# The opening's squares, the constants' conversion and the early products of a fp32 decoder layer, put in another order

## The chip, the cores and the metric

One NeuronCore of a Trainium2 chip runs the whole layer as one program. The time is that of one execution on the device, in microseconds (us). Five engines work beside each other, each through its own queue in program order, and wait for one another by semaphores: PE (TensorE, matrix products; PEld is its loading of weights), DVE (VectorE), ACT (ScalarE), POOL (GpSimd) and SP (SyncE, which here only issues DMAs). POOL issues some DMAs too.

## What is computed

A decoder layer on x of 1024 positions by 1024 features, all in fp32, with a D_FF of 2816:

```
x = x + 0.5 * swiglu_ffn(rmsnorm(x, ffn1_norm), ffn1_w_gate, ffn1_w_up, ffn1_w_down)
x = x + hybrid_mixer(rmsnorm(x, mix_norm), ...)      # NSA attention + gated linear attention
x = x + 0.5 * swiglu_ffn(rmsnorm(x, ffn2_norm), ffn2_w_gate, ffn2_w_up, ffn2_w_down)
return rmsnorm(x, final_norm)

swiglu_ffn(x, w_gate, w_up, w_down) = (silu(x @ w_gate) * (x @ w_up)) @ w_down
rmsnorm(x, g) = x * rsqrt(mean(x * x) + EPS) * g
```

## The kernel before

**Products.** Each fp32 product is three matmuls on rounded halves (`mm3`, L193 to L195: high by high, high by low, low by high). A weight tile is brought from DRAM to `raw` by SP (L407 for the early ones), its high half is made by ACT (L433) and its low half by DVE (L436). Making weights is a `step` of the walk over the list of products, which looks up to four products ahead (`LOOK`).

**FFN.** The hidden features are worked through in 22 tiles of 128. For each the up and gate products over two halves of x (positions and features both cut in two) are formed by a scheme of Strassen's kind: seven products of 12 matmuls each, of sums and differences of the weights (S1 to S4, DVE) with sums and differences of the halves of x (T1 to T4). One of the seven, A12 by B21, needs only features 4 to 7 of x in half 0 of the positions, multiplied by the gain but not yet by the norm; so these **early products** are done for all 22 tiles ahead of the tiles. The result of each is copied by ACT from PSUM to a half of `kept` (even and odd tiles alternate, L612), stored by SP to the DRAM buffer `pd` (L546), and brought back (`recall`, L546 too) when its tile comes, where DVE adds it (L640) to the snapped A11 product `hf`. A copy to a half of `kept` waits until the store that reads that half has landed.

**Opening.** While the early products run, ACT and DVE make the norm of x: eight squares for each half of the positions (ACT L248), added up by DVE (L252, the last one L257), summed over the partitions by PE (L268), then v (DVE L273), its power of -0.5, r (POOL L275), and r spread over the partitions by PE (L280); for half 0 ACT copies that to SBUF (`rb`, L1934). Then DVE scales x in place (16 times, L304), the halves of x are made (ACT L312 the highs, DVE L313 the lows), and `combine` makes the differences (DVE L334) for T2, T3, T1 and T4 and their halves. All this is a side generator (`first`): it gets one tick behind each k-step of a product, that is behind every 3 matmuls, and a table `due` of ticks says when the steps of the norm are emitted; `PACE` sets how fast the combinations follow. What one engine does in which order is thus settled by the order in which the code emits it.

**FFN2.** Its opening is emitted in the mixer's last loop over the output (`ot`, L2149 adds to x, L248 squares, L2158 stores x to `xs`), with the early weights loaded by `ahead` and a `step` at two of the places.

**Constants.** `round_consts` has POOL convert two DRAM tables of 2.1 MB each (`qx`, `bias`) to the rounded type by DMA from DRAM to DRAM (L114). They are needed in the mixer.

## Time and profile before

| | |
|---|---|
| median of 3 runs | 1945.82 us (1945.74 to 1947.72) |
| the profiled execution | 1946.0 us, span 1944.2 us |
| PE busy | 1909.6 us, 98% of the span |
| DVE, ACT, POOL busy | 70%, 46%, 11% |
| matmuls | 9291 |
| granted TensorE clock, mean | 0.993 |

In the rows of the timeline and of the groups the first number is the start in us, the second the time in us (busy time for a group), then engine, line, operation, output <- inputs by the program's names, tile shapes, and xN for N instructions in a row. In brackets: how long the engine was idle just before, and whose end it waited for. Lines are those of the kernel before. In the table of DMA issues the last number is the median from issue to landing.

### The profile page before, as it was taken

Reading aid. Unit: us, or ns where it says so; the run is one execution under the profiler, and the core shown is the slowest. Engines: PE = TensorE matmul, PEld = TensorE weight load, DVE = VectorE, ACT = ScalarE, POOL = GpSimd, SP = SyncE. Lnnn points to the kernel's source line nnn. Section 1 sums busy time; section 2 is a strip of 40 time slices with the busy share of each in tenths; the row PEclk is TensorE's granted clock in tenths of the full one; section 3 lists DMA queues with packets and bytes.
Section 4 is the critical chain, followed back from the end, with each engine's and each line's share of the span. In section 5 each row is a group of like instructions: output and inputs, shape, how many; then the busy total and the mean of one; then the engine's idle time right before and its main releaser. Section 6 shows DMA issues by size and latency. Waiting matters only on the chain.

```text
span 1944.2 us, 26337 instructions
## 1 busy us (share of the span) xinstructions
PE 1909.6 (98%) x9291; PEld 1569.5 (81%) x9291; DVE 1370.5 (70%) x2292; ACT 898.1 (46%) x1717; POOL 219.8 (11%) x251
## 2 busy tenths in 40 slices
PE   8899999999999999999999999999999999999998
PEld 6788888888888888778877888878788888888887
DVE  6887778886776763454867887457777777767766
ACT  5533333344444552323479887235433333344443
POOL 0000000000000010121467654000000000000001
PEclk9999999999999999999999999999999999999999
DMA  8533345559874330118353422635333455588652
GB/s 292 186 131 127 128 152 193 192 195 335 298 254 163 124 102 27 53 46 243 128 168 94 148 71 93 227 122 192 125 130 130 152 195 195 195 308 284 237 177 87
DMA packets 173588, 325.53 MB, mean 167 GB/s; under 512 B 17712, under 2 KB 49072, under 8 KB 173136
## 3 DMA queue, kind: packets, MB, share of 16 engines
q1 hardware_dynamic: 165296, 308.87, 46.8%
q0 software_dynamic: 2304, 10.23, 1.6%
q10 hardware_dynamic: 5856, 4.75, 0.8%
q8 instruction: 73, 1.20, 0.2%
q14 instruction: 59, 0.48, 0.1%
HBM read 234.75 MB, written 93.39 MB: 169 GB/s over the span
## 4 chain that ended last, share of the span: by engine, by line
PE 88%; DVE 4%; ACT 3%; DMA 3%; issue 1%; POOL 1%; SPq 0%; ACTq 0%; POOLq 0%; DVEq 0%
PE bank L193 23%; PE bank L194 23%; PE bank L195 23%; PE pair L1431 3%; PE bank L1503 3%; PE bank L963 2%; PE bank L965 2%; PE bank L964 2%; PE bank L1521 1%; PE bank L1522 1%; DMA raw<-in_w_f_dram 1%; ACT p L1472 1%; DMA pd<-kept 1%; PE bank L1156 0%; PE pair L1439 0%
## 5 line engine op out<-in xcount | busy, mean ns | idle before, releaser
L193 PE MATMUL bank<-T,wt 128*128 128x512 f32 x704 | 275.0, 391 | 7.0 <-ACT hf L612 6.6
L194 PE MATMUL bank<-T,wt 128*128 128x512 f32 x704 | 274.6, 390 | 0.0
L195 PE MATMUL bank<-T,wt 128*128 128x512 f32 x704 | 274.5, 390 | 0.0
L193 PE MATMUL bank<-bd,wd 128*128 128x512 f32 (+1 forms) x632 | 243.1, 385 | 0.0
L195 PE MATMUL bank<-bd,wd 128*128 128x512 f32 (+1 forms) x632 | 242.6, 384 | 0.0
L194 PE MATMUL bank<-bd,wd 128*128 128x512 f32 (+1 forms) x632 | 242.5, 384 | 0.0
L193 PE MATMUL bank<-h,wt 128*128 128x512 f32 x528 | 208.0, 394 | 0.5 <-ACT wt L433 0.5
L195 PE MATMUL bank<-h,wt 128*128 128x512 f32 x528 | 206.7, 392 | 0.4 <-DVE wt L436 0.3
L194 PE MATMUL bank<-h,wt 128*128 128x512 f32 x528 | 206.7, 391 | 0.0
L275 POOL TENSOR_TENSOR r<-v,mhalf 128x4 f32<-128x4 f32 (+1 forms) x9 | 10.4, 1159 | 1355.2 <-DVE v L273 1355.2
L612 ACT ACTIVATE g<-bank 128x512 f32<-128x512 f32 x88 | 52.7, 598 | 236.3 <-PE bank L195 236.3
L193 PEld LDWEIGHTS bank<-T,wt 128*128 128x128 f32 x704 | 132.6, 188 | 35.7 <-ACT hf L612 7.5
L195 PEld LDWEIGHTS bank<-T,wt 128*128 128x128 f32 x704 | 132.6, 188 | 27.6
L194 PEld LDWEIGHTS bank<-T,wt 128*128 128x128 f32 x704 | 132.6, 188 | 27.6
L433 ACT ACTIVATE wt<-v 128x512 fp32r<-128x512 f32 x176 | 109.9, 624 | 76.7 <-PE bank L195 50.9
L193 PEld LDWEIGHTS bank<-bd,wd 128*128 128x128 f32 x632 | 118.8, 188 | 23.5
L195 PEld LDWEIGHTS bank<-bd,wd 128*128 128x128 f32 x632 | 118.7, 188 | 23.4
L194 PEld LDWEIGHTS bank<-bd,wd 128*128 128x128 f32 x632 | 118.8, 188 | 23.2
L193 PE MATMUL bank<-h,w 128*128 128x512 f32 x320 | 127.2, 398 | 0.0
L195 PE MATMUL bank<-h,w 128*128 128x512 f32 x320 | 124.9, 390 | 0.0
L436 DVE TENSOR_TENSOR wt<-v,wt 128x512 fp32r<-128x512 f32 x176 | 120.6, 685 | 6.0 <-ACT wt L433 5.6
L194 PE MATMUL bank<-h,w 128*128 128x512 f32 x320 | 124.7, 390 | 0.0
(279 smaller groups left out, 3883.8 us busy)
## 6 DMA issues: line engine op xcount, KB each, us to landing
in<-in_w_f_dram SPq DMA_DIRECT2D x132, 256.0 KB, 5.4
in<-b SPq DMA_DIRECT2D x132, 256.0 KB, 5.4
raw<-in_w_f_dram SPq DMA_DIRECT2D x44, 512.0 KB, 4.6
up<-in_w_f_dram SPq DMA_DIRECT2D x44, 512.0 KB, 5.3
raw<-in_w_in_dram SPq DMA_DIRECT2D x23, 512.0 KB, 4.0
raw<-in_w_f_dram SPq DMA_DIRECT2D x44, 256.0 KB, 3.9
pd<-kept SPq DMA_DIRECT2D x44, 256.0 KB, 2.2
kept<-pd SPq DMA_DIRECT2D x44, 256.0 KB, 5.7
```

What stands on the lines that cost most here:

```text
L193: mm(ps, w[0], x[0], start=first, stop=False, skip_group_check=True)
L194: mm(ps, w[0], x[1], start=False, stop=False, skip_group_check=True)
L195: mm(ps, w[1], x[0], start=False, stop=last, skip_group_check=True)
L433: nc.scalar.activation(t[:, 0], a, AF.Copy)
L436: nc.vector.tensor_tensor(t[:, 1], a, t[:, 0].bitcast(F32), OP.subtract)
L612: nc.scalar.activation(dst, src, AF.Copy)
L963: mm(p, a, w[:, 0, c], start=f, stop=False, skip_group_check=True)
L964: mm(p, a, w[:, 1, c], start=False, stop=False, skip_group_check=True)
L965: mm(p, b, w[:, 0, c], start=False, stop=l, skip_group_check=True)
L1431: nc.tensor.matmul(s[:, i + c, :w], Q[:, j, r], kk[br, g][:, k0:k0 + w], start=(j == 0 and i % per == 0), stop=False, skip_group_check=True)
L1472: nc.scalar.activation(p[:, i].rearrange("p (c w) -> p c w", c=nch), sv[:, i * nch:i * nch + nch], AF.Exp, bias=nm[:, i:i + 1], accum_out= ...
L1503: nc.tensor.transpose(t[:, r * 128:r * 128 + 128], heads[r][:, k * 128:k * 128 + 128], self.ident)
```

## The change

- **Opening.** `begin` takes two steps of weights more and then emits six of the eight squares of half 0 ahead of the first products; the other two come at the side generator's ticks 1 and 2. The squares of half 1 begin at tick 20 instead of 10. The steps of the norm come at ticks 19, 23, 31 and 35 (before: 18, 22, 25 and 29), the scalings and combinations from tick 27 on (before 24). `PACE` goes from 1.35 to 1.3. For the first two products the look-ahead is three.
- **Constants.** `round_consts` is called 16 times, behind the A22 products of tiles 4 to 19, each time for an eighth of `qx` or `bias`. Ahead of each DMA POOL copies a column of the weights of a tile five ahead into a fifth column of `mhalf`, so that the DMA, behind the copy in POOL's queue, is issued once these weights have landed. Before, the two DMAs were written behind tile 10's A22, but no operand made them wait.
- **Early products.** They go through tiles 2 to 21 and then 0 and 1 (`head`). The results of tiles 0 and 1 stay in `kept`: they are not stored to `pd` and not brought back.
- **FFN2.** `ahead(0)` and `ahead(1)` are called behind `ot` 5 and `ahead(2)` behind `ot` 7; before, `ahead(0)` behind 5 and the other two behind the loop.

```diff
 AHEAD2 = 12
-PACE = 1.35
+PACE = 1.3
...
         self.gains = self.const.tile([128, 4, KT], F32, name="gains")
-        self.mhalf = self.const.tile([128, 4], F32, name="mhalf")
+        self.mhalf = self.const.tile([128, 5], F32, name="mhalf")
         self.blank = self.const.tile([128, 128], BF, name="blank")
...
-    def round_consts(self):
-        for n in ("qx", "bias"):
-            src = self.ins[f"c_{n}"]
-            t = self.dram.tile(list(src.shape), R32, name=n)
-            self.nc.gpsimd.dma_start(t, src)
-            setattr(self, n, t)
+    def round_consts(self, i, after):
+        n, b = ("qx", "bias")[i % 2], i // 2
+        src = self.ins[f"c_{n}"]
+        if not b:
+            setattr(self, n, self.dram.tile(list(src.shape), R32, name=n))
+        self.nc.gpsimd.tensor_copy(self.mhalf[:, 4:], after)
+        self.nc.gpsimd.dma_start(getattr(self, n)[b], src[b])
...
         E, H = {}, []
+        head = list(range(2, D)) + list(range(min(D, 2)))
         minus = lambda o, p, q: nc.vector.tensor_tensor(o, p, q, OP.subtract)
...
-        def ahead(j, parts=(0, 1)):
+        def ahead(n, parts=(0, 1)):
+            j = head[2 * n] // 2
             if j not in E:
...
                 if early(f, q):
-                    if f % 2 or f == D - 1:
+                    if f % 2:
+                        n = head.index(f) // 2
                         E.pop(f // 2)
-                        if f + 5 < D:
-                            ahead(f // 2 + 3)
-                        elif f // 2 == (D - 1) // 2 - 2:
+                        if n + 3 < D // 2:
+                            ahead(n + 3)
+                        elif n == D // 2 - 3:
                             load(0)
...
             def mm():
-                ps = [one(f) for f in range(2)]
+                ps = [one(f) for f in (2, 3)]
                 for k in range(4):
                     ks = slice(k * 128, k * 128 + 128)
-                    for f in range(2):
+                    for f in (2, 3):
                         wt, bt = W[f, "A12"], B["21"]
-                        self.mm3(ps[f], (wt[:, 0, ks], wt[:, 1, ks]), (bt[k][:, 0], bt[k][:, 1]), k == 0, k == 3)
+                        self.mm3(ps[f - 2], (wt[:, 0, ks], wt[:, 1, ks]), (bt[k][:, 0], bt[k][:, 1]), k == 0, k == 3)
                         if self.idle:
...
                         self.tick()
-                for f in range(2):
+                for f in (2, 3):
                     self.free(W.pop((f, "A12")))
-            for f in range(2):
-                seq.append(((f, "A12"), lambda kinds, f=f: ready(f, "A12", kinds), mm if f else lambda: None,
-                            (lambda: [save(f)() for f in range(2)]) if f else None))
+            for f in (2, 3):
+                seq.append(((f, "A12"), lambda kinds, f=f: ready(f, "A12", kinds), mm if f == 3 else lambda: None,
+                            (lambda: [save(f)() for f in (2, 3)]) if f == 3 else None))
...
                 snap(t, Z.pop(f))
-                send(pd[f], t)
-                if f == D - 1:
-                    recall(0)
+                if f > 1:
+                    send(pd[f], t)
             return post
         def recall(f):
-            if f < D:
+            if 1 < f < D:
                 send(kept()[:, f % 2], pd[f])
...
                 first2()
-            for f in range(2 * begun, D):
+            for f in head[2 * begun:]:
                 product(f, "A12", "21", lambda f=f: one(f), True, True, save(f))
...
             for i, (key, _, mm, post) in enumerate(seq):
-                while at_[0] < len(seq) and at_[0] <= i + LOOK and step(i):
+                while at_[0] < len(seq) and at_[0] <= i + LOOK - (i < 2) and step(i):
                     pass
...
                 pos[0] += 1
-                if key[0] == FT - 1 and key[1] in gone:
+                if key[1] in gone and key[0] == (head[-1] if D and key[1] == "A12" else FT - 1):
                     self.free(*B.pop(gone[key[1]]))
...
             nc.vector.tensor_scalar(ss, ss, 4.0 / 128, 4.0 * EPS, op0=OP.mult, op1=OP.add)
-            nc.gpsimd.tensor_tensor(ss, ss, self.mhalf, OP.pow)
+            nc.gpsimd.tensor_tensor(ss, ss, self.mhalf[:, :4], OP.pow)
             og = self.nt.tile([128, 512], F32, name="sq").rearrange("p (h t) -> p h t", h=4)
...
                     settle()
+            for _ in range(2):
+                step()
+            settle()
+            for k in (4, 5, 6, 7, 0, 1):
+                square(0, k)
+        def square(half, k):
+            self.squares(ns[half], x, slice(half * 512, half * 512 + 512), k, nc.vector, "hf" if half else "acc")
...
-            due = {18: lambda: go_on(0), 22: lambda: go_on(0), 25: lambda: go_on(1), 29: lambda: go_on(1),
-                   23: lambda: nc.scalar.activation(rb[:, 0], ns[0]["rb"], AF.Copy)}
-            for n, (half, k) in enumerate([(0, k % KT) for k in range(4, 12)] + [(1, k) for k in range(KT)]):
-                t = n if n < 8 else 10 + (n - 8) * 5 // 4
-                while clock[0] < t:
+            due = {19: lambda: go_on(0), 23: lambda: go_on(0), 31: lambda: go_on(1), 35: lambda: go_on(1),
+                   24: lambda: nc.scalar.activation(rb[:, 0], ns[0]["rb"], AF.Copy)}
+            for n, (half, k) in enumerate([(0, 2), (0, 3)] + [(1, k) for k in range(KT)]):
+                while clock[0] < (1 + n if n < 2 else 20 + (n - 2) * 6 // 5):
                     yield
...
                         due.pop(clock[0])()
-                self.squares(ns[half], x, slice(half * 512, half * 512 + 512), k, nc.vector, "hf" if half else "acc")
-                if n % 8 == 7:
+                square(half, k)
+                if n in (1, 9):
                     self.total(ns[half], nc.vector)
...
                     due.pop(clock[0])()
-                if clock[0] > 23:
+                if clock[0] > 26:
                     try:
...
         self.open_banks(False)
-        hooks1 = {"post": post, "x": again(ins["xT"]), (10, "A22"): self.round_consts, "begun": True,
+        hooks1 = {"post": post, "x": again(ins["xT"]), "begun": True,
                   ("2", 3, 2): lambda: self.raws(0), ("3", 0): lambda: self.later(2),
                   (FT - 1, "S1"): lambda: self.free(rms_of[0])}
+        for i in range(16):
+            hooks1[i + 4, "A22"] = lambda i=i: self.round_consts(i, raws[i + 5][0][:, :1])
         step, settle, go = self.ffn(w1, B, lambda: rms_of[0][:, 0], 0, 5, loader(w1), raws, hooks1, FT)
...
                     ahead(0)
+                    ahead(1)
+                if half and ot == 7:
+                    ahead(2)
                 if half and ot in (7, 0):
...
         self.unring()
-        ahead(1)
-        ahead(2)
         self.hold = (4, "A12")
```

How this moves the engines' instructions is shown at three places. Lines after `combine`'s helpers are one to a dozen higher in the changed kernel: L252 becomes L253, L257 L258, L273 L274, L304 L305, L433 L436, L436 L439, L612 L615, L1934 L1945, L2149 L2161, L2158 L2170, L407 L410 and L546 L549. A row is line, operation, output <- inputs, tile, and xN for N of it in a row.

**The opening on DVE**, from the last add of half 0's squares to the first scaling of x. `acc` is the sum of half 0, `hf` and `sq` here that and the squares of half 1, `wt` the lows of weights. Before:

```order
L257 TENSOR_TENSOR acc<-acc,sq 128x512
L436 TENSOR_TENSOR wt<-raw,wt 128x512 x2
L252 TENSOR_TENSOR hf<-hf,sq 128x512 x3
L436 TENSOR_TENSOR wt<-raw,wt 128x512
L252 TENSOR_TENSOR hf<-hf,sq 128x512 x2
L273 TENSOR_SCALAR v<-bank 128x4
L252 TENSOR_TENSOR hf<-hf,sq 128x512
L257 TENSOR_TENSOR hf<-hf,sq 128x512
L436 TENSOR_TENSOR wt<-raw,wt 128x512 x2
L304 SCALAR_TENSOR_TENSOR x<-x,gains,bank 128x512
```

The same stretch of the changed kernel:

```order
L258 TENSOR_TENSOR acc<-acc,sq 128x512
L439 TENSOR_TENSOR wt<-raw,wt 128x512 x4
L274 TENSOR_SCALAR v<-bank 128x4
L439 TENSOR_TENSOR wt<-raw,wt 128x512
L253 TENSOR_TENSOR hf<-hf,sq 128x512 x2
L439 TENSOR_TENSOR wt<-raw,wt 128x512
L253 TENSOR_TENSOR hf<-hf,sq 128x512 x3
L439 TENSOR_TENSOR wt<-raw,wt 128x512
L253 TENSOR_TENSOR hf<-hf,sq 128x512
L258 TENSOR_TENSOR hf<-hf,sq 128x512
L305 SCALAR_TENSOR_TENSOR x<-x,gains,bank 128x512 x2
```

The five adds of half 1 that stood ahead of v now stand behind it, and the first two scalings of x stand together behind the sum of half 1. From the second scaling to the first difference for T4 there are 67 instructions in both.

**The opening on ACT**, ahead of `rb`, from the copy of the third early product on. Before:

```order
L612 ACTIVATE kept<-bank 128x512
L433 ACTIVATE wt<-raw 128x512
L248 ACTIVATE sq<-x 128x512 x3
L612 ACTIVATE kept<-bank 128x512
L433 ACTIVATE wt<-raw 128x512
L248 ACTIVATE sq<-x 128x512 x3
L612 ACTIVATE kept<-bank 128x512
L433 ACTIVATE wt<-raw 128x512
L1934 ACTIVATE rb<-bank 128x512
```

And in the changed kernel, from the fourth early product's copy to half 1's last square:

```order
L615 ACTIVATE kept<-bank 128x512
L436 ACTIVATE wt<-raw 128x512
L615 ACTIVATE kept<-bank 128x512
L436 ACTIVATE wt<-raw 128x512
L249 ACTIVATE hf<-x 128x512
L249 ACTIVATE sq<-x 128x512 x3
L615 ACTIVATE kept<-bank 128x512
L436 ACTIVATE wt<-raw 128x512
L1945 ACTIVATE rb<-bank 128x512
L249 ACTIVATE sq<-x 128x512 x3
L615 ACTIVATE kept<-bank 128x512
L436 ACTIVATE wt<-raw 128x512
```

One more square of half 1 follows these. The squares of half 1 have moved from ahead of `rb` to both sides of it, behind more copies of `kept`. On PE the first L268 stands behind 60 matmuls of products (before 57) and the first L280 behind 72 (69); for half 1 it is 96 and 108 (78 and 90). The first T product stands at the same place.

**FFN2's opening on SP**, around the last stores of x (`xs`). Before:

```order
L2158 DMA xs_11511<-x 128x2x512 x4
L407 DMA raw<-in_w_f_dram 128x512 x2
L2158 DMA xs_11511<-x 128x2x512
L407 DMA raw<-in_w_f_dram 128x512 x2
L2158 DMA xs_11511<-x 128x2x512
L407 DMA raw<-in_w_f_dram 128x512 x4
L546 DMA pd<-kept 128x512 x2
```

After:

```order
L2170 DMA xs_11537<-x 128x2x512 x4
L410 DMA raw<-in_w_f_dram 128x512 x4
L2170 DMA xs_11537<-x 128x2x512
L410 DMA raw<-in_w_f_dram 128x512 x4
L2170 DMA xs_11537<-x 128x2x512
L549 DMA pd<-kept 128x512 x2
```

The four loads that stood behind the last store of x stand ahead of it. On DVE the last addition to x, the last square's add, a low of weights, the sum (L257) and v followed each other; now the low stands behind v:

```order
L2161 TENSOR_TENSOR x<-x,bank 128x512
L253 TENSOR_TENSOR acc<-acc,sq 128x512
L258 TENSOR_TENSOR acc<-acc,sq 128x512
L274 TENSOR_SCALAR v<-bank 128x4
L439 TENSOR_TENSOR wt<-raw,wt 128x512 x4
```

Of one low ahead of the sum and three behind v, all four are now behind v, and with them the wait of that low for its high and its load.

## The prediction

> **What bounds the kernel now.** I read the first two parts of the page, then the waits by engine, then windows for the slices in which the row of PE falls below 9. A window row gives start:end, its length, the busy time (and instructions) of PE, PEld, DVE, ACT and POOL, the granted clock, the DMA share and GB/s; a wait row gives who waited for whom, the total, how often, and the longest.
>
> ```profile
> span 1944.2 us, 26337 instructions
> PE 1909.6 (98%) x9291; PEld 1569.5 (81%) x9291; DVE 1370.5 (70%) x2292; ACT 898.1 (46%) x1717; POOL 219.8 (11%) x251
> ...
> PE bank L193 <- ACT hf L612: 6.6, 2, 5.9
> ...
> PE bank L280 <- POOL r L275: 5.5, 3, 4.9
> ...
> PE bank L268 <- DVE acc L257: 4.0, 2, 3.4
> ...
> 20.00:40.00 20.00, 14.56 (x72) 11.98 (x71) 13.97 (x25) 14.12 (x26) 3.76 (x4) 0.91 0.71 239
> 80.00:100.00 20.00, 14.06 (x55) 11.16 (x54) 17.11 (x29) 12.62 (x23) 0.00 (x0) 0.83 0.47 158
> 100.00:300.00 200.00, 200.00 (x884) 165.63 (x883) 151.68 (x237) 76.81 (x135) 0.00 (x0) 1.00 0.40 140
> 1280.00:1320.00 40.00, 36.57 (x156) 30.46 (x155) 20.03 (x32) 14.49 (x26) 1.40 (x1) 0.91 0.50 165
> ```
>
> PE is the bound. Where it is full (100:300) it makes 884 matmuls in 200 us, **0.226 us each**, so a product of 12 lasts 2.7 us. The change removes no matmul; what it can win is idle or slow PE. Three stretches have that: 20 to 40 us (5.4 idle, clock 0.91), 80 to 100 (5.9 idle, 0.83) and 1280 to 1320 (3.4 idle, 0.91). The three wait rows say who is late there: the first norm's r, the chain of combinations ahead of the T products, and the sum of squares of FFN2. The change touches all three.
>
> **Opening, half 0.**
>
> ```profile
> 21.66 1.05 PE L268 MATMUL bank<-ones,acc 128*128 128x1 f32 x8 [0.57 <-DVE acc L257]
> 23.45 0.60 ACT L612 ACTIVATE kept<-bank 128x512 f32<-128x512 f32 x1 [0.24 <-DMA pd<-kept]
> 23.94 0.62 ACT L433 ACTIVATE wt<-raw 128x512 fp32r<-128x512 f32 x1
> 26.52 0.68 DVE L436 TENSOR_TENSOR wt<-raw,wt 128x512 fp32r<-128x512 f32 x1
> 28.64 0.15 DVE L273 TENSOR_SCALAR v<-bank 128x4 f32<-128x4 f32 x1
> 28.87 1.52 POOL L275 TENSOR_TENSOR r<-v,mhalf 128x4 f32<-128x4 f32 x1 [28.44 <-DVE v L273]
> 30.45 1.72 PE L280 MATMUL bank<-ident,r 128*128 128x128 f32 x8 [4.88 <-POOL r L275]
> ```
>
> PE's sums (L268) were in at 22.7, yet v came only at 28.64: ahead of it in DVE's queue stood five adds of half 1, each waiting for a square on ACT. In the new order no square of half 1 stands there, only four lows of weights. The last of them needs the third `kept` copy, which still waits for the store of the first (23.45, +0.60), then its high (+0.62) and itself (0.68): v about 25.1, r 1.5 later, L280 about **26.7**. PE does three matmuls more ahead of L268 and does not wait 0.57: L268 at 21.66 - 0.57 + 0.68 = 21.8, and after it and a product it stands at L280 at 21.8 + 0.8 + 2.7 = 25.3. A wait of 1.4 stays of 4.88, and L280 itself lasts some 0.8 (1.72 now, at the halved clock).
>
> **Opening, half 1.**
>
> ```profile
> 35.11 0.95 PE L268 MATMUL bank<-ones,hf 128*128 128x1 f32 x8
> 35.92 0.48 PE L193 MATMUL bank<-h,wt 128*128 128x512 f32 x1
> 36.17 0.74 DVE L304 SCALAR_TENSOR_TENSOR x<-x,gains,bank 128x512 f32<-128x512 f32 x1
> ```
>
> The eight squares of half 1 now follow. From 24.7 ACT has 17 operations up to the last square (four kept, four highs, the copy rb, eight squares) of 0.57 to 0.6 each: about 34.5; two adds on DVE make the sum at about 35.6. PE, 24 matmuls behind L280, is there at 26.7 + 0.8 + 5.4 = 32.9. So PE gets a **new wait of some 2.7 us** where it had none, and L268 takes its 0.8 slot (35.11 to 35.92) about 35.6. The first two scalings of x (L304) stand behind that sum on DVE, so the second is at about 36.3: 36.17 before. What the faster half 0 won is held by half 1.
>
> **Combinations and the constants.**
>
> ```profile
> 37.30 0.75 POOL L114 DMA_DIRECT2D qx<-in_c_qx_dram  x1
> 52.79 0.60 ACT L612 ACTIVATE kept<-bank 128x512 f32<-128x512 f32 x1 [10.37 <-DMA pd<-kept]
> 53.94 0.69 DVE L436 TENSOR_TENSOR wt<-raw,wt 128x512 fp32r<-128x512 f32 x1 [6.88 <-ACT wt L433]
> 36.17:86.04 49.87, 46.15 (x206) 37.64 (x205) 42.09 (x68) 27.05 (x51) 2.24 (x3) 0.99 0.70 240
> 86.04 1.89 DVE L334 TENSOR_TENSOR x<-x 128x512 f32<-128x512 f32 x3
> 87.90 0.58 ACT L612 ACTIVATE hf<-bank 128x512 f32<-128x512 f32 x1
> 88.53 0.79 PE L193 MATMUL bank<-T,wt 128*128 128x512 f32 x1 [5.93 <-ACT hf L612]
> 88.53:92.34 3.81, 3.81 (x9) 3.03 (x10) 1.87 (x3) 0.45 (x1) 0.00 (x0) 0.50 0.83 252
> ```
>
> From 36.17 to the first subtraction for T4 (86.04) DVE runs 67 instructions, in both orders: 42.09 busy in 49.87, and 6.88 of the rest is one wait: the two big conversions were issued from 37.3 us on, a store of `kept` behind them landed late, ACT stood 10.37 and DVE with it. In the new order POOL's first copy waits for a tile's weights, so nothing of the constants moves here, and the 6.88 goes. T2's product starts at 88.53 - 6.88 + 0.1 = **81.75, a gain of 6.8**. PE gets there sooner too: L280 of half 1, now after 108 matmuls instead of 90, ends at 35.6 + 0.8 + 2.7 + 0.8 = 39.9 against 39.5; before it reached T2 at 88.53 - 5.93 = 82.6, now at 82.6 + 0.4 - 18 x 0.226 = 78.9. So a **wait of 2.85 remains**. After the old one the clock was 0.50 for 3.81 us, 1.9 lost. I take the remaining waits (1.4, 2.7, 2.85) as too short for that: the shortest wait I see with a slow stretch behind it is the 3.43 at FFN2, below. The rows don't exclude that 2.85 is enough; then the gain is 1.9 less. Gain of the opening: 6.8 + 1.9 = **8.7**; nothing is added for the clock at 31 us, as that lies ahead of the second scaling.
>
> The Trainium skill, "TensorE: Matmul & The Clock Gate", in its part on the clock gate, has the clock halve after a whole idle window of some 3.4 us, on windows that run freely. The trace agrees as far as it goes (3.43, 4.88 and 5.93 idle were each followed by a slow stretch). By the page the opening is worth 8.7, and the 6.8 without the clock is out as long as the waits stay under 3.4; by the rows alone either could be.
>
> The 16 pieces go out between tiles 4 and 19, a sixteenth of the bytes each. A tile is six products, 16.3 us, so this is about 82.6 + 5 x 16.3 = 164 to 82.6 + 20 x 16.3 = 409 us, somewhat sooner where the weights that a piece waits for come ahead of their tile. There PE never waits and the DMA share is 0.40 (100:300). I take 0. From below: nothing can be gained there. From above: the whole cost 10.37 of ACT when it came at once, 0.65 for a piece, which PE does not see where DVE has 48 of 200 us free. POOL's 16 copies and issues stand ahead of no other work until the mixer.
>
> **FFN2's opening.**
>
> ```profile
> 1290.86 0.38 SPq L2158 DMA_DIRECT2D xs<-x  x1
> 1290.93 0.63 ACT L248 ACTIVATE sq<-x 128x512 f32<-128x512 f32 x1 [4.30 <-DVE x L2149]
> 1291.33 2.27 SPq L407 DMA_DIRECT2D raw<-in_w_f_dram  x4
> 1295.61 1.28 ACT L433 ACTIVATE wt<-raw 128x512 fp32r<-128x512 f32 x2 [4.05 <-DMA raw<-in_w_f_dram]
> 1296.80 0.58 ACT L612 ACTIVATE kept<-bank 128x512 f32<-128x512 f32 x1
> 1296.88 0.68 DVE L257 TENSOR_TENSOR acc<-acc,sq 128x512 f32<-128x512 f32 x1
> 1297.62 1.87 PE L268 MATMUL bank<-ones,acc 128*128 128x1 f32 x8 [3.43 <-DVE acc L257]
> 1303.62 0.68 PE L193 MATMUL bank<-h,wt 128*128 128x512 f32 x1
> ```
>
> The weights were issued behind the last store of x, came at 1295.6, and the sum of squares stood behind their low on DVE. Now they are issued before that store, and the sum stands ahead of the lows: the last square ends at 1291.6, the sum by 1292.9, before PE comes (1297.62 - 3.43 = 1294.2). L268 at about 1294.1, v 1295.0, r (1.5) to 1296.6, L280 at 1296.8 with PE there at 1296.3; it ends at 1297.6. The next product's weights are now behind two kept copies (1296.4 and 0.58) and a high and low (0.62, 0.7) after them: 1298.2, so 0.6 of new wait. At full clock its first matmuls save 0.28: 1303.62 + 0.28 - 1298.2 = **5.7**. No rows show SP's issues in the new place; with the weights late by 1 us after all it would be 4.7, with no new waits 6.7.
>
> **Tiles 0 and 1 kept.**
>
> ```profile
> 1363.00 0.69 DVE L640 TENSOR_TENSOR hf<-kept,hf 128x512 f32<-128x512 f32 x1 [2.08 <-DMA kept<-pd]
> ...
> 1368.03 0.50 PE L193 MATMUL bank<-T,wt 128*128 128x512 f32 x1 [0.42 <-ACT g L612]
> ...
> pd<-kept SPq DMA_DIRECT2D x44, 256.0 KB, 2.2
> kept<-pd SPq DMA_DIRECT2D x44, 256.0 KB, 5.7
> ```
>
> Two stores and two loads less in each FFN. The first recall made DVE wait 2.08 at FFN2's first tile, and of that chain PE felt 0.42 at 1368.03: I count **0.4**, between 0 and 1.0. In FFN1 the T chain covers it.
>
> **Sum.** 8.7 + 5.7 + 0.4 = 14.8. The profiled execution took 1946.0 (span 1944.2 and 1.8 around it): 1931.2. The median shown is 1945.8, 0.2 less, so **1931**.
>
> **Rivals.**
> 1. *Half 1 does not hold the opening*: ACT and the stores run faster than I have them. If the sum of half 1 comes 2.7 sooner, no wait is left there and T2 comes 2.7 sooner: 1931 - 2.7 = 1928.3. If nothing at all waits, 4.88 + 5.93 + 0.57 + 1.9 and the clock's 1.8 of 20:40 (0.09 of 20) go, 15.1 with FFN2's 6.1: **1924.6**. For it: in 20:40 ACT is busy 14.12 of 20, so it has slack. Against: 17 operations stand between v and the sum, and DVE's 42.09 busy behind it would have to begin near 31 us. I give it the time 1927.
> 2. *The opening keeps more*: the stores of `kept` land late (the loads of the same size take 5.7 where the stores take 2.2; one of 3.5 more on the chain ahead of half 1's sum). T2 comes 3 us later, the waits before it grow past 3.4 and the clock halves: 8.7 - 3 - 1.9 = 3.8, with 6.1 gives **1935.9**. Only the halving: 1932.9, in my forecast.
> 3. *The pieces are not held*: POOL goes through its queue as early as before. For it nothing but the weights being loaded ahead; then 6.88 and 1.9 return: 14.8 - 8.7 = 6.1, **1939.7**.
> 4. *Slower: the pieces hurt where PE is full.* Each piece delays a tile's weights or its store and recall, and with them the ring that feeds PE. At 0.65 a piece they would cost 10.4 together if nothing covered them; from 0.92 (14.8 / 16) the gain is gone, from 1.17 it is slower by 0.2%; at 1.3, twice the old burst, 20.8: **1952**. Against: PE's 200.00 of 200.00 with 884 matmuls while 140 GB/s went by, 2.3 MB in the 16.3 us between two pieces, beside which a piece (16 x 4096 values, 0.26 MB) is little.
>    The Trainium skill, "DMA: Bandwidth & Descriptors", in its part on queues, rings and completion order, speaks for this rival: a transfer's completion is a write that lands only behind all earlier writes of its DMA engine, whatever their queue. The 10.37 of a small store behind the big conversions agrees. By it each piece holds up every store and load issued behind it.
>
> **How the numbers follow.** Forecast 0.55 (1929 to 1933.5), rival 1 0.22, rival 2 0.17, rival 3 0.03, rival 4 0.03. The likeliest gives 1931. The range takes in most of rivals 1 and 2: 1926 to 1936. 0.2% is 3.9 us, about what can be told from no change here: faster (below 1941.9) is the forecast and rivals 1 to 3, and rival 4 is split between same and slower: 0.95, 0.03, 0.02.
>
> **What would show it.** In the profile after: PE's wait for r at 26 us near 1, the clock at 1.00 through 20:40; a new wait of L268 for hf of 2 to 3 us at 33; the 10.37 before `kept` gone; the first matmul of bank<-T at 81 to 82 with a wait of 2 to 3.4 and the clock at 1.00 after it; pieces of qx and bias between 140 and 410 us with PE full around them; at 1294 no wait of 3.43 but two of about 0.5. Wrong would make it: a half clock after a wait I have below 3.4, or losses between 140 and 410 us.

## The result, and the profile after

The changed kernel takes 1931.68 us (median of 4 runs, 1930.06 to 1932.15) where the kernel before, timed beside it, takes 1946.48 (1945.74 to 1947.72): a ratio of 0.9922, 95% interval 0.9905 to 0.9939. That is 14.8 us, the sum that was forecast. The profiled execution is the fastest of the four (1930.06, span 1928.3), so the times by stage below add up to 15.9, not to 14.8. One run of x10 below took 5183.58 us at a granted clock of 1.00; it stands apart from the other three, is not in that kernel's median, and its cause is not known.

The head of the page:

```profile
span 1928.3 us, 26353 instructions
...
PE 1904.2 (99%) x9291; PEld 1566.9 (81%) x9291; DVE 1370.0 (71%) x2292; ACT 897.6 (47%) x1717; POOL 229.0 (12%) x281
```

The windows of the stages; the columns are a window's ends, its length, busy time of PE, PEld, DVE, ACT and POOL, the granted clock, the DMA share and GB/s:

```profile
20.00:40.00 20.00, 16.69 (x89) 13.73 (x88) 12.80 (x22) 13.83 (x26) 2.47 (x2) 1.00 0.53 191
80.00:100.00 20.00, 20.00 (x89) 16.54 (x89) 17.71 (x29) 9.30 (x17) 0.00 (x0) 1.00 0.19 65
100.00:300.00 200.00, 200.00 (x884) 165.59 (x883) 152.31 (x238) 75.91 (x134) 7.06 (x20) 1.00 0.46 157
1270.00:1310.00 40.00, 39.80 (x183) 32.56 (x182) 25.11 (x40) 16.63 (x30) 1.02 (x1) 1.00 0.51 171
```

All three weak stretches are at full clock now; one of them is full (20.00 of 20.00) and one nearly so (39.80 of 40.00). Between 100 and 300 us PE makes the same 884 matmuls with the first ten pieces of the constants beside it. The other six go out between 301.86 and 383.42 us, and from 300 to 400 us PE is full too, with 443 matmuls before and after. So the pieces cost it nothing. The opening on the timeline:

```profile
21.51 0.95 PE L269 MATMUL bank<-ones,acc 128*128 128x1 f32 x8
22.89 0.60 ACT L615 ACTIVATE kept<-bank 128x512 f32<-128x512 f32 x1 [2.06 <-DMA pd<-kept]
24.64 0.16 DVE L274 TENSOR_SCALAR v<-bank 128x4 f32<-128x4 f32 x1
25.96 1.16 PE L281 MATMUL bank<-ident,r 128*128 128x128 f32 x8 [0.62 <-POOL r L276]
35.27 1.05 PE L269 MATMUL bank<-ones,hf 128*128 128x1 f32 x8 [2.69 <-DVE hf L258]
35.79 0.74 DVE L305 SCALAR_TENSOR_TENSOR x<-x,gains,bank 128x512 f32<-128x512 f32 x1
39.03 1.05 PE L281 MATMUL bank<-ident,r 128*128 128x128 f32 x8
77.23 1.89 DVE L335 TENSOR_TENSOR x<-x 128x512 f32<-128x512 f32 x3
79.72 0.50 PE L194 MATMUL bank<-T,wt 128*128 128x512 f32 x1 [1.52 <-ACT hf L615]
136.10 0.75 POOL L117 DMA_DIRECT2D qx<-in_c_qx_dram  x1
```

The wait for r has shrunk from 4.88 to 0.62. The new wait for half 1's sum is there with 2.69 (2.7 was forecast), and the first T product comes at 79.72 instead of 88.53 behind a wait of 1.52. From 35.79 to 77.23 DVE's rows in this stretch show no idle time at all: its 67 instructions now are the chain.

A measure by stage, used for all kernels below: the start of the same matmul by its number in PE's order, before minus after. No. 3000 lies ahead of the mixer (694.2 us before), 6300 ahead of FFN2's opening (1265.5), 6460 behind that (1306.6), and 6760 behind the first recall (1376.3).

| one profiled execution of each | 3000 | 6300 | 6460 | 6760 | span |
|---|---|---|---|---|---|
| changed kernel | 10.6 | 8.7 | 14.6 | 15.3 | 15.9 |
| x1 constants at once | -0.6 | -2.0 | 3.8 | 4.5 | 5.1 |
| x2 constants whole, held | 9.0 | 9.0 | 14.8 | 15.5 | 16.1 |
| x3 squares as before | 7.5 | 7.2 | 13.0 | 13.8 | 14.4 |
| x10 FFN2, both as before | 7.0 | 5.9 | 7.6 | 8.3 | 9.0 |
| x4 FFN2, loads as before | 8.8 | 3.8 | 9.6 | 10.4 | 10.4 |
| x9 FFN2, hold as before | 9.1 | 8.5 | 14.7 | 15.4 | 16.0 |
| x13 tiles in order | 8.6 | 7.2 | 13.3 | 13.4 | 13.4 |
| x5 sum of half 1 sooner | 6.6 | 4.4 | 10.2 | 11.0 | 11.6 |
| x6 sum of half 1 later | 7.1 | 5.7 | 11.5 | 12.3 | 12.9 |
| x7 lows on POOL | 6.5 | 4.2 | 10.0 | 10.8 | 10.7 |
| x11 three squares sooner | 10.9 | 8.2 | 14.0 | 14.8 | 14.7 |
| x12 x11 and x7 | 10.8 | 9.8 | 15.6 | 16.3 | 16.0 |

A negative number is a loss. So the changed kernel's 15.9 is 10.6 in the opening (all that lies ahead of No. 3000), -1.8 in the mixer, which the change doesn't touch, 5.8 in FFN2's opening, 0.7 at its first tile and 0.6 at the end. In x2, x4, x9 and x10 the opening's instructions are those of the changed kernel; with it these are five executions of one opening: 10.6, 9.1, 9.0, 8.8 and 7.0. The forecast for it was 8.7.

### The profile page after: what moved, and what is told of

Its sections match the earlier page's. It is cut to its first block, busy times and chain, and to the rows that moved or that the text cites. A ratio compares the mean times of both kernels' runs of the same rounds, so it can differ in the third digit from the quotient of the medians.

```text
span 1928.3 us, 26353 instructions
## 1 busy us (share of the span) xinstructions
PE 1904.2 (99%) x9291; PEld 1566.9 (81%) x9291; DVE 1370.0 (71%) x2292; ACT 897.6 (47%) x1717; POOL 229.0 (12%) x281
## 5 line engine op out<-in xcount | busy, mean ns | idle before, releaser
L615 ACT ACTIVATE g<-bank 128x512 f32<-128x512 f32 x88 | 52.7, 598 | 244.0 <-PE bank L196 244.0
L436 ACT ACTIVATE wt<-v 128x512 fp32r<-128x512 f32 x176 | 109.8, 624 | 68.9 <-PE bank L196 39.5
L439 DVE TENSOR_TENSOR wt<-v,wt 128x512 fp32r<-128x512 f32 x176 | 120.7, 686 | 5.4 <-ACT wt L436 5.1
```

Source lines behind the costliest of these rows:

```text
L436: nc.scalar.activation(t[:, 0], a, AF.Copy)
L439: nc.vector.tensor_tensor(t[:, 1], a, t[:, 0].bitcast(F32), OP.subtract)
L615: nc.scalar.activation(dst, src, AF.Copy)
```

## The experiments

All edits are to the changed kernel; ratios are to the kernel before, run beside them, with their 95% intervals. Line numbers of a kernel can differ by one or two from those of the changed kernel.

### The constants: at once, or whole but held

x1 gives back the two whole DMAs that nothing holds:

```diff
-        for i in range(16):
-            hooks1[i + 4, "A22"] = lambda i=i: self.round_consts(i, raws[i + 5][0][:, :1])
+        hooks1[10, "A22"] = self.round_consts
```

> All of the change but the constants, which go as before in two whole DMAs that nothing holds. Theory (the conversions cost the opening its stall of DVE, and the new order of the squares doesn't help against it): the DMAs go out behind the second r at about 38 us, ACT waits about 10 us for a store of kept, DVE some 7; the first T product starts at 86 to 88 us instead of 79.7, behind a wait of 7 to 9 and with a slow stretch of the clock after it; total about 1931.7 + 6.9 + 1.9 = 1940.5 (1938.5 to 1942.5). Rival (the order of the squares is what gained): T at about 80, total 1932.

x2 sends the two tables whole as well, each behind POOL's copy of a weight column:

```diff
-        n, b = ("qx", "bias")[i % 2], i // 2
+        n = ("qx", "bias")[i]
...
-        self.nc.gpsimd.dma_start(getattr(self, n)[b], src[b])
+        self.nc.gpsimd.dma_start(getattr(self, n), src)
...
-        for i in range(16):
+        for i in range(2):
```

> The constants in two whole DMAs again, but each held by a copy of a weight tile as in the changed kernel (two instead of 16, at 136 and 153 us). Theory (only the moment counts): PE stays full from 130 to 180 us, total 1931.7 within 1. Rival (the size of a burst counts wherever it comes, so the 16 pieces are needed): stores, recalls and weights land some 10 us late, PE loses 2 to 10 us between 136 and 180, total 1934 to 1942.

x1 took 1941.07 us (8 runs, 1940.04 to 1942.35; 0.9971, 0.9960 to 0.9982), x2 1932.26 (4 runs, 1929.87 to 1935.15; 0.9928, 0.9913 to 0.9942). The timeline of x1:

```profile
38.53 0.75 POOL L114 DMA_DIRECT2D qx<-in_c_qx_dram  x1
54.45 0.60 ACT L613 ACTIVATE kept<-bank 128x512 f32<-128x512 f32 x1 [11.21 <-DMA pd<-kept]
55.60 0.69 DVE L437 TENSOR_TENSOR wt<-raw,wt 128x512 fp32r<-128x512 f32 x1 [9.01 <-ACT wt L434]
89.26 0.79 PE L192 MATMUL bank<-T,wt 128*128 128x512 f32 x1 [7.68 <-ACT hf L613]
```

The old stall is back, even longer than expected (DVE 9.01, before 6.88), and with it T at 89.26, where 86 to 88 was expected, and the slow clock: the opening gains nothing (-0.6 in the table). **Without the held constants the new order of the squares is worth nothing.** And the window of x2 in which its two whole DMAs go out (137.79 and 154.65 us):

```profile
130.00:190.00 60.00, 60.00 (x267) 49.67 (x266) 45.00 (x70) 21.63 (x38) 1.58 (x4) 1.00 0.60 210
```

PE is full there, as the theory had it. What counts here is the moment, not the size of a piece: one copy in front of each whole DMA would have done.

### The opening's order

x3 undoes it alone (squares, ticks, pace, and the look-ahead of FFN1):

```diff
-            for _ in range(2):
-                step()
-            settle()
-            for k in (4, 5, 6, 7, 0, 1):
-                square(0, k)
...
-            due = {19: lambda: go_on(0), 23: lambda: go_on(0), 31: lambda: go_on(1), 35: lambda: go_on(1),
+            due = {18: lambda: go_on(0), 22: lambda: go_on(0), 25: lambda: go_on(1), 29: lambda: go_on(1),
...
-            for n, (half, k) in enumerate([(0, 2), (0, 3)] + [(1, k) for k in range(KT)]):
+            for n, (half, k) in enumerate([(0, k % KT) for k in range(4, 12)] + [(1, k) for k in range(KT)]):
```

> All of the change but the opening's order: squares, due ticks, pace and look-ahead of FFN1 as before. Theory (behind the second scaling of x DVE is the bound of the opening, and that scaling is as late in both orders, so the order of the squares only frees PE): T could start at 36.2 + 41.4 + 2.5 = 80.1, but PE, with the wait of 4.9 for r and its slow clock back, gets there at 82.6; so T at about 82.6 with no wait and no slow stretch after it, 2.9 later than in the changed kernel: total about 1934.6 (1933.5 to 1936). Rival (the order of the squares carries the opening): T at 88, total about 1940.

1933.09 us (1931.61 to 1933.51; 0.9930, 0.9915 to 0.9945), 0.4 below the range of its theory and 1.4 above the changed kernel's median, with overlapping intervals; in its trace:

```profile
29.88 2.07 PE L281 MATMUL bank<-ident,r 128*128 128x128 f32 x8 [4.83 <-POOL r L276]
82.68 0.50 PE L194 MATMUL bank<-T,wt 128*128 128x512 f32 x1 [0.69 <-ACT hf L615]
```

The whole wait for r (4.83) is back, yet T comes at 82.68, as worked out, with 0.69 of wait: PE catches up, since DVE's chain would have kept it waiting anyway. In the table the opening is 7.5, against 7.0 to 10.6: 1.5 less than the middle of the five (9.0), 3 less than the best. As 7.5 lies among the five, neither this execution nor the medians show that the order of the squares is worth anything beyond the spread.

Two kernels move the sums of half 1 in PE's queue, two ticks sooner (x5) and four later (x6):

```diff
-            due = {19: lambda: go_on(0), 23: lambda: go_on(0), 31: lambda: go_on(1), 35: lambda: go_on(1),
+            due = {19: lambda: go_on(0), 23: lambda: go_on(0), 29: lambda: go_on(1), 33: lambda: go_on(1),
```

x6 has 35 and 39 there.

> The sums of half 1 on PE two ticks (6 matmuls) sooner in PE's queue. Theory: PE waits there 2.7 + 1.4 = 4.1 us until the same sum at about 35.3; the clock then halves for certain (it did behind 2.5 in two runs and didn't behind 2.7 in one), the second L281 comes 2 to 3 us later, the scalings of half 1 with it, and T starts at 82 to 84: total 1934 to 1936. Rival (the wait lies beside DVE's chain, which alone sets T): T at 79.7 to 80.5, total 1932.

> The sums of half 1 on PE four ticks (12 matmuls) later in PE's queue, so that their squares are summed just when PE comes. Theory (DVE's chain is the bound up to T, and PE's waits only change places): no wait and no slow clock at 32 to 40 us, the second L281 still at 39, T at 79.7 as before, behind a wait of 1.5 + 2.7 = 4.2 that is followed by a slow stretch of 1.9: total 1932.5 to 1934. Rival (PE's wait at the sum was itself lost time): T 2.7 sooner at 77, total 1929.

x5: 1933.96 us (1932.38 to 1935.40; 0.9932, 0.9916 to 0.9949). x6: 1933.42 (1933.11 to 1933.74; 0.9931, 0.9916 to 0.9945). First x5's rows, then x6's:

```profile
35.43 1.87 PE L269 MATMUL bank<-ones,hf 128*128 128x1 f32 x8 [3.95 <-DVE hf L258]
41.98 1.05 PE L281 MATMUL bank<-ident,r 128*128 128x128 f32 x8
83.64 0.50 PE L194 MATMUL bank<-T,wt 128*128 128x512 f32 x1 [1.12 <-ACT hf L615]
```

```profile
36.59 1.05 PE L269 MATMUL bank<-ones,hf 128*128 128x1 f32 x8 [0.84 <-DVE hf L258]
43.96 2.08 PE L281 MATMUL bank<-ident,r 128*128 128x128 f32 x8 [3.46 <-POOL r L276]
83.20 0.50 PE L194 MATMUL bank<-T,wt 128*128 128x512 f32 x1 [1.12 <-ACT hf L615]
```

x5's T came as its theory said, and its total at the edge of the range, but the way was in part another: v now stands ahead of the first two scalings on DVE and waits for PE's slow sum, so the second scaling starts at 38.07 instead of 35.79. For x6 the total lies in the theory's range, but not for the theory's reason. The sums and v are emitted at the same tick, so with later sums v stands behind more scalings on DVE, and PE waits 3.46 for r instead. Its second scaling, too, is 1.3 late (37.11), which its edit doesn't explain: ACT waited 1.87 us for a store of `kept` at 27.34, where it waits 1.01 in the changed kernel. In both the second L281 is 3 to 5 late and T 3.5 to 3.9. By the table (6.6 and 7.1 for 7.0 to 10.6) neither place is better than the changed kernel's.

### FFN2's opening

The trace of the changed kernel has no wait at its L269 (1285.28 to 1286.23) and 5.8 gained. Two things differ there: the loads, and the order on DVE. The order isn't made by the lines at `ot` 5 and 7. The line `self.hold = (4, "A12")` stops the look-ahead at tile 4; with tiles 2 and 3 first, tile 4 is the third early product, where it was the fifth, so one `step` fewer is taken ahead of the sum. x10 undoes both, x4 the loads alone, x9 the hold alone:

```diff
                     ahead(0)
-                    ahead(1)
-                if half and ot == 7:
-                    ahead(2)
...
         self.unring()
+        ahead(1)
+        ahead(2)
-        self.hold = (4, "A12")
+        self.hold = (6, "A12")
```

> All of the change but FFN2's opening: the loads behind the last store of x as before, and the look-ahead held at the fifth early product as before (with the tiles' new order the hold at tile 4 had become the third). Theory: the low ahead of the sum and its late load are back, PE waits about 3.4 at L269 with a slow stretch after it: FFN2's opening loses 6, total about 1937.8 (1936.8 to 1938.8). Rival (the stage gains by something else, the tiles kept on chip): 1932.

> Of FFN2's opening only the loads go back behind the last store of x; the order on DVE (sum ahead of the lows) stays new. Theory (the loss needs both: a low ahead of the sum, and its load late): L269 doesn't wait, since the sum needs no weights; the loads land some 4 us after the store's issue, in time for the product behind L281; the stage loses 0 to 0.5, total 1931.7 to 1932.3. Rival (the loads carry the gain): 3.1 to 3.4 of wait and a slow stretch, total 1937.8.

> Of FFN2's opening only the hold goes back to the fifth early product, so that a low stands ahead of the sum on DVE; the loads stay ahead of the last store of x. Theory (both are needed for the loss): the weights are there by then, the low costs DVE 0.7, the sum still comes before PE; the stage loses 0 to 1, total 1931.7 to 1932.7. Rival (the order on DVE carries the gain): total 1937.8.

x10: 1938.18 us (three runs, 1937.02 to 1938.35; 0.9956, 0.9939 to 0.9972), as its theory said. x4: 1932.84 (1931.03 to 1935.65; 0.9929, 0.9914 to 0.9944). x9: 1930.09 (1929.65 to 1933.90; 0.9918, 0.9903 to 0.9933). Of these two medians the first is 0.5 above the range of its theory and the second 1.6 below; both are far from the rivals' 1937.8, and the stage decides. The rows of x10, then the L269 of x4 and of x9:

```profile
1289.41 1.29 ACT L436 ACTIVATE wt<-raw 128x512 fp32r<-128x512 f32 x2 [3.73 <-DMA raw<-in_w_f_dram]
1290.68 0.69 DVE L258 TENSOR_TENSOR acc<-acc,sq 128x512 f32<-128x512 f32 x1
1291.42 1.05 PE L269 MATMUL bank<-ones,acc 128*128 128x1 f32 x8 [3.11 <-DVE acc L258]
```

```profile
1290.21 0.95 PE L269 MATMUL bank<-ones,acc 128*128 128x1 f32 x8
```

```profile
1285.55 0.95 PE L269 MATMUL bank<-ones,acc 128*128 128x1 f32 x8
```

Between No. 6300 and 6460 x10 gains 1.7, x4 5.8, x9 6.2 and the changed kernel 5.8. **Either edit alone is enough.** The wait needs a low ahead of the sum and late weights under that low; with one of the two gone the sum is ready when PE comes. That x10 still gains 1.7 is the clock's doing: behind its wait of 3.11 it is halved for 3.41 us (1292.42 to 1295.84), in the kernel before for 6.83 (1297.22 to 1304.05), and half of the difference is 1.7.

### The tiles kept on chip

x13 takes the early products in order again and stores and recalls tiles 0 and 1:

```diff
-        head = list(range(2, D)) + list(range(min(D, 2)))
+        head = list(range(D))
...
-                if f > 1:
-                    send(pd[f], t)
+                send(pd[f], t)
+                if f == D - 1:
+                    recall(0)
...
-            if 1 < f < D:
+            if f < D:
```

> All of the change but the early products' order: tiles 0 to 21 in order, the results of tiles 0 and 1 stored to pd and recalled as before (the hold at tile 4 is then the fifth product again, which alone cost nothing beside the new loads). Theory (the recall of tile 0 is late only at FFN2's first tile): DVE waits about 2 us for kept ahead of tile 0's add there and PE loses 0.4 to 0.5 once, nothing in FFN1; by the stage 0.5, total 1931 to 1933. Rival (the traffic of four transfers an FFN matters around the T products): T in FFN1 1 to 3 later, total 1934.

1932.44 us (1930.98 to 1934.50; 0.9929, 0.9912 to 0.9945): within the range of its theory, and not told apart by its time. By the stage it gains 0.1 between No. 6460 and 6760, where all other kernels gain 0.7: keeping the two tiles is worth 0.6 to 0.7, once, in FFN2 (one execution without it). T in FFN1 is at 81.68, among the five of the same opening.

### Can the opening be shorter?

If ACT's chain sets the sum of half 1 and DVE's chain sets T, then squares sooner and less work for DVE should help. x11 puts three squares of half 1 into the gaps of ACT at 18 to 22 us, x7 has POOL make eight lows, x12 has both:

```diff
-                while clock[0] < (1 + n if n < 2 else 20 + (n - 2) * 6 // 5):
+                while clock[0] < (1 + n if n < 2 else 7 + n if n < 5 else 20 + (n - 5) * 6 // 5):
...
-                nc.vector.tensor_tensor(t[:, 1], a, t[:, 0].bitcast(F32), OP.subtract)
+                eng = nc.gpsimd if "begun" in hooks and early(f, q) and f % 2 == 0 and head.index(f) > 4 else nc.vector
+                eng.tensor_tensor(t[:, 1], a, t[:, 0].bitcast(F32), OP.subtract)
```

x11 and x12 also have half 1's steps at ticks 30 and 34.

> The changed kernel with three of half 1's eight squares moved ahead of the third copy of kept, where ACT stands idle twice for about 2 us (for a weight load and for a store), and the norm of half 1 one tick sooner. Theory (ACT's chain behind v sets the sum of half 1, that sum sets the start of DVE's chain, and a shorter wait at L269 leaves the clock whole): the sum at 33.5 instead of 35.2 to 35.9, PE's wait at L269 1 to 1.8 without a slow stretch, T at 77.5 to 79 instead of the 81.2 to 81.5 of x2, x4 and x9; total 1928 to 1930. Rival (stores of kept, not the squares, set ACT's time): the sum stays at 35, total 1931 to 1932.

> The changed kernel with the lows of eight early weights (every other tile from tile 8 on, and tile 0) made on POOL instead of DVE. Theory (behind the second scaling DVE has no idle time, so its work is the length of the chain): some six lows less on DVE ahead of T, 4 us; T comes when PE does, at 78 to 79.5; total 1928.5 to 1930.5. Rival (POOL's pass is slower, and disturbs DVE or holds up the early products): lows of 0.9 to 2 us each, PE waits for them, T no sooner; total 1931 to 1935.

> Both edits of the two kernels beside it: three squares sooner and eight lows on POOL. Theory: with the sum sooner and DVE's chain shorter PE is the bound; T at 76.5 to 78 with a wait of 0 to 1; total 1926.5 to 1929. Rival (POOL's lows cost what they save): as with the squares alone or worse, 1929 to 1933.

x11: 1930.13 us (5 runs, 1928.09 to 1932.90; 0.9909, 0.9896 to 0.9923). x7: 1934.06 (1933.52 to 1935.68; 0.9931, 0.9919 to 0.9944). x12: 1931.32 (1930.40 to 1931.83; 0.9915, 0.9901 to 0.9928). None can be told from the changed kernel's 0.9922 (0.9905 to 0.9939). Rows of x11's timeline, the window behind them, and the group of lows on POOL in x7 (busy time and mean ns of one behind the bar):

```profile
33.25 1.05 PE L269 MATMUL bank<-ones,hf 128*128 128x1 f32 x8 [0.97 <-DVE hf L258]
79.33 0.50 PE L194 MATMUL bank<-T,wt 128*128 128x512 f32 x1 [0.89 <-ACT hf L615]
```

```profile
34.60:38.00 3.40, 3.40 (x10) 2.62 (x9) 3.40 (x7) 2.34 (x5) 1.39 (x1) 0.51 0.21 80
```

```profile
L440 POOL TENSOR_TENSOR wt<-raw,wt 128x512 fp32r<-128x512 f32 x8 | 11.3, 1414 | 43.3 <-ACT wt L436 43.3
```

In x11 the sum came 2 us sooner, as its theory said, but the clock halved all the same, and T missed the 77.5 to 79 of the theory. T, at 79.33, is 0.4 sooner than in the profile of the changed kernel and about 2 sooner than in x2, x4 and x9, and the 10.9 of its opening is above all five; but the mixer took 2.7 back in that execution, so the total shows no gain. x12, with the same squares, kept a whole clock and still had T at 79.49 behind a wait of 1.87, not at 76.5 to 78: its rival held.

A low takes POOL 1.41 us where DVE takes 0.69, and in x7 the rival's numbers came: the wait at L269 grew to 3.88 and T came at 83.72. But most of that sum's lateness isn't the lows'. The third copy of `kept` on ACT waits for a store, first in the changed kernel, then in x10, whose opening is the same, then in x7:

```profile
26.03 0.60 ACT L615 ACTIVATE kept<-bank 128x512 f32<-128x512 f32 x1 [1.01 <-DMA pd<-kept]
26.75 0.60 ACT L615 ACTIVATE kept<-bank 128x512 f32<-128x512 f32 x1 [1.86 <-DMA pd<-kept]
27.07 0.60 ACT L616 ACTIVATE kept<-bank 128x512 f32<-128x512 f32 x1 [1.90 <-DMA pd<-kept]
```

That copy is 0.7 later in x10 and 1.0 in x7, and PE's sum (L269) 0.7 and 1.3. So x7 doesn't tell what the lows on POOL alone would cost.

## Why the prediction was right, by its steps

- **Constants: right, and the largest term.** x1 shows that the stall of DVE belongs to them; taking them out of the opening is worth 9.6 there (9.0 less -0.6). That the pieces cost nothing is shown by the full windows; that pieces aren't needed, by x2.
- **Half 0: right, too long by 0.8.** The wait was 0.62 for the 1.4 taken: v came at 24.64 for 25.1, and r took 1.0, not 1.5. (The four terms that the prediction names for v add up to 25.35, not 25.1; nothing in the sum hangs on it.)
- **Half 1: right.** A wait of 2.69 for 2.7, the second scaling at 35.8 for 36.3.
- **T at 81.75: right for three of five executions, in part by luck.** The profile of the change has 79.72; x2, x4 and x9, with the same opening, have 81.25, 81.50 and 81.16, x10 83.25. The wait of PE ahead of T was 1.1 to 1.5, not 2.85. In the profile of the change that is because T came 2.0 sooner (PE was there at 78.2, for 78.9); in the four others PE came later, at 80.0 to 82.1, by the next step.
- **"I take the remaining waits as too short for that": this step failed.** It held at L281 and at T, and in the profile of the change, but behind the sum of half 1 the clock halved in all four other executions of the opening, behind waits of 2.26, 2.51, 2.54 and 3.52 (only the last is as long as the 3.43 that the prediction took as the shortest). A row of x9's timeline and the window behind it:

```profile
35.55 1.05 PE L269 MATMUL bank<-ones,hf 128*128 128x1 f32 x8 [2.26 <-DVE hf L258]
```

```profile
36.47:41.70 5.23, 5.23 (x23) 4.29 (x22) 5.23 (x10) 3.81 (x8) 1.45 (x1) 0.67 0.29 90
```

  The clock is 0.50 from 36.95 to 40.36 there. The second L281 then comes at 40.7 to 42.7 instead of 39.0, and T at 81.16 to 83.25 instead of 79.72. The 1.9 that the sum counted for the clock at T was gained; what it left out is a half clock of 3.41 us at the sum (6.83 in x10), which costs PE 1.7 us (3.4). T hangs on DVE's chain, from the second scaling to the difference. The sum took it as 43.0, its length in the old order. It was 42.6 in x2, x4 and x9 and 44.2 in x10, and 41.4 in the profile of the change, where the clock stayed whole. So the forecast hit the middle of the opening (9.0 for 8.7) by luck in part: it saw neither the slow clock nor the shorter chain, and the two nearly cancel. That the slow clock is what lengthens the chain is likely from these five, but no run shows it alone.
- **FFN2: size right (5.8 for 5.7), reason half.** Of the two new waits of about 0.5 that it counted, PE had about 0.2 at each place. The two causes were named together and counted once; x4 and x9 show that each alone suffices. That the order on DVE came from the hold, and so from the tiles' order, was not seen.
- **Tiles kept: right.** 0.4 taken, 0.6 to 0.7 measured.
- **Left out: the mixer.** Between No. 3000 and 6300 the same instructions lost 1.8 in the changed kernel, 0.1 in x2 and 5.0 in x4, and the end gained 0.6 in some and nothing in others. The half-clock stretches of the mixer differ too (from 3.41 to 13.65 us together), but don't settle it: x7 has 3.41, as before, and lost 2.3. Such differences also part runs of one kernel: x4's lie between 1931.0 and 1935.7.
- **Rivals.** The first (half 1 doesn't hold the opening) was the profile of the change in its size, not by its cause: the wait of 2.7 was there. The second came true in x10's opening in part: a store landed late (ACT's copy at 26.75 for 26.03), the wait at the sum grew to 3.52, the clock halved, and T came at 83.25, 1.8 to 2.1 behind x2, x4 and x9. The third is x1's price. The fourth didn't occur.

## What to carry to other kernels

A bulk transfer that nothing holds goes out at the first moment its queue is free, here into the tightest 50 us of the program; one cheap instruction on the issuing engine, reading a tile that lands later, moves it, and cutting it up added nothing. Taking away a wait of PE is worth what the next chain leaves of it: the 4.8 at r made 1.4 of difference in the medians, within their spread, since T hung on DVE's chain. The five executions of one opening gained 7.0 to 10.6, so a single profile doesn't tell orders of this kind apart. After a renumbering look for constants that name a number: the hold at tile 4 moved an engine's order without its line being touched.

## What the runs showed of the hardware

The granted clock halved behind shorter waits than any that it followed in the profile of before, and not behind all of the same length: it stayed whole behind 2.69 in the changed kernel and behind 1.28 in x12, and halved behind 2.26 in x9 and behind 0.97 in x11 (0.51 from 34.6 to 38.0 us). Each of these waits ended in L269, 8 matmuls of one column each that last 1.05 us, so the stretch without wide matmuls was about 2.0 us in x11, 3.3 in x9 and 3.7 in the changed kernel. Behind the waits ahead of T (0.69 to 1.87 us in x2 to x13), which a wide matmul ends, it halved in none. The Trainium skill, "TensorE: Matmul & The Clock Gate", in its part on the clock gate, asks for a whole idle window of some 3.4 us; x11, in which PE was idle 0.97 us and then made narrow matmuls, doesn't agree.

The traces show more of what decides it. In each of the 14 the granted clock changes only at moments that lie a whole number of 3.41 us apart, so they form a grid, and where the grid lies differs from execution to execution. What counted in the openings is the share of one stretch of the grid in which PE made matmuls other than the one-column ones. Two neighbouring stretches of the changed kernel, one of x11 and one of x9 (the first number behind the comma is PE's busy time, one-column matmuls included, and the clock is that of the stretch itself):

```profile
31.07:34.49 3.42, 1.51 (x7) 0.93 (x5) 2.59 (x4) 3.18 (x6) 0.00 (x0) 1.00 0.70 234
34.49:37.90 3.41, 2.63 (x16) 2.33 (x17) 3.38 (x7) 1.26 (x2) 1.22 (x1) 1.00 0.16 59
31.23:34.65 3.42, 2.45 (x15) 1.90 (x14) 2.71 (x5) 2.00 (x5) 0.00 (x0) 1.00 0.65 229
33.54:36.95 3.41, 1.40 (x10) 1.36 (x11) 3.19 (x7) 1.97 (x5) 0.00 (x0) 1.00 0.29 106
```

Without the one-column matmuls the shares are 0.44, 0.50, 0.45 and 0.14; the clock stayed whole behind the first two and halved behind the others. Over the openings of both FFNs in all traces, from 20 us on, it halved behind each full-clock stretch with 0.39 or less (15 of them) and behind none with 0.50 or more. At 0.44 to 0.45 it stayed whole twice and halved once. So the 2.69 of the changed kernel did no harm because a boundary, at 34.49, cut it in two, which is luck of the execution; the 2.26 of x9 lay in one stretch. In the mixer, whose matmuls are of other kinds, the clock halved at shares up to 0.71, so the limit isn't one of time alone.
